# The first blocks of an encoder layer in an order held on every engine: pieces of 256 and 384 columns, three weights, zeros ahead

## The chip, the core and the metric

One core of a Trainium2 chip runs the whole kernel. The metric is the device time of one execution in microseconds (us). PE is the matrix engine (PEld its weight loads), DVE the vector engine, ACT the scalar engine, POOL the general one, and SP the engine whose queue issues the DMAs. Each engine takes its instructions in the order in which they stand in its queue.

## What is computed

One layer over 1024 prompt rows and 128 sample rows (8 streams of 16), 1152 rows of 1024 numbers in float32. The start, which the change is about, is the norm and the input projection:

```python
h = rmsnorm(x, g_pre_mix)
p = h @ w_in                       # 4352 columns
qa, ka, va, qb, kb, vb, ga, gb = jnp.split(p, cuts, axis=-1)
...
oa = prompt_band(qa, ka, va, ...)  # window attention, 8 heads on 2 KV heads
ob = prompt_band(qb, kb, vb, ...)  # chunk-band attention, 8 heads
merged = jax.nn.sigmoid(ga) * (oa @ w_oa) + jax.nn.sigmoid(gb) * (ob @ w_ob)
x = x + rmsnorm(merged @ w_out, g_post_mix)
f, conv_new = conv_ffn(rmsnorm(x, g_pre_ffn), conv_buf, w_upg, conv_w, conv_b, w_down)
return x + rmsnorm(f, g_post_ffn), ...
```

## The kernel before

Rows are taken in nine blocks of 128 (tb 0 to 8; the last holds the samples). For each block the beginning does the same seven things: a load of x (512 KB), a square with its sum on ACT (L162), the reciprocal root on POOL in two small instructions (L103, L104), the scaled block xn on DVE (L165), eight transposes on PE into two PSUM tiles `tp` (L135), and for each of these a high part of hT on ACT (L137) and a low part on DVE (L138). Operands are kept as a rounded high part and the rest, so each product is three: high by high, high by low, low by high (`mm3`, L125 to L127). A weight of 1024 x 128 is loaded raw, its high part is made on ACT (L108) and its low part on DVE (L111).

hT is held in two parts: part 0 is blocks 0 to 4 (640 columns), part 1 blocks 5 to 8 (512), each as two tiles of four k-blocks. A projection of one weight is done in three pieces of columns, `PIECES`: 320 and 320 of part 0, and 512 of part 1. A piece is 24 products into one PSUM tile, which ACT evacuates (L226; for a gate weight L302). The weights are ka and va, then q0, then for each of eight units of attention those of the next unit, with pieces of 16 gate weights (g0 to g15) dealt out over the units by `gates_per_unit`. Inside a unit the steps of attention and the dense pieces alternate. After the attention come the second merge, the output projection, and the convolutional MLP with a fast matrix scheme.

The order on each engine is made by a scheduler from the program's text and its dependences. In the kernel before it is free everywhere, and it takes ka and va alone into the beginning; the biases (`bias_tables`, one small product of PE, L533) and the constants on POOL and DVE stand where it puts them. `piece`, `weight_tile`, `split_w` and `transpose_to` are the helpers that the change touches.

```python
for g in range(NP):
    run(first[g], first[NP + g])
    if g == 0:
        bias_tables()
run(*first[2 * NP:])
```

`first` holds the pieces of ka, va and q0; `run` records all of a piece at once.

Of the kernel before, what the change touches and what calls it, by code (L numbers as in the profile page):

```python
# [11 lines left out]
F32 = mybir.dt.float32  # L12
F32R = mybir.dt.float32r
# [5 lines left out]
P = 128  # L19
D = 1024  # L20
# [24 lines left out]
def fr(ap):  # L45
    return ap.bitcast(F32)
# [3 lines left out]
def encoder_step(ctx, tc, x, w_in, w_o, w_out, w_upg, w_down, kc, vc, state_conv, conv_w, conv_b,  # L50
# [50 lines left out]
    def rstd_of(ss, out, eng=nc.vector):  # L101

        eng.tensor_scalar(out, ss, 1.0 / D, EPS, op0=ALU.mult, op1=ALU.add)  # L103
        nc.gpsimd.tensor_tensor(out, out, nhalf[:, 0:out.shape[1]], op=ALU.pow)  # L104

    def split_w(raw, sp, hi_engine="scalar", lo_engine="gpsimd"):
        if hi_engine == "scalar":
            nc.scalar.activation(sp[:, 0], raw[:], AF.Copy)  # L108
        else:
            nc.vector.tensor_copy(sp[:, 0], raw[:])  # L110
        getattr(nc, lo_engine).tensor_tensor(sp[:, 1], raw[:], fr(sp[:, 0]), op=ALU.subtract)  # L111

    def weight_tile(src, name, hi_engine="scalar"):
        raw = wr.tile([P, KD, P], F32, name=f"{name}r", tag="wr")
        nc.sync.dma_start(raw[:], src)
        sp = ws.tile([P, 2, KD, P], F32R, name=f"{name}s", tag="ws")
        split_w(raw, sp, hi_engine, "vector")
        return sp

    def mm3(ps, w, x, cols, k0, nk, start=True, stop=True):  # L120

# [7 lines left out]
    def transpose_to(pool_ps, src, dst, tb):  # L129

        s, c = part_of(tb)
        for q in range(2):
            pt = pool_ps.tile([P, 4, P], F32, name=f"tp{tb}_{q}", tag="pt")
            for k in range(4):
                nc.tensor.transpose(pt[:, k], src[:, (4 * q + k) * P:(4 * q + k + 1) * P], ident[:])  # L135
            hi = dst[s][q][:, 0, :, c:c + P]
            nc.scalar.activation(hi, pt[:], AF.Copy)  # L137
            nc.vector.tensor_tensor(dst[s][q][:, 1, :, c:c + P], pt[:], fr(hi), op=ALU.subtract)  # L138
# [6 lines left out]
    with ExitStack() as ph:  # L145
# [5 lines left out]
        early = {}  # L151
        with ExitStack() as pre:
            xp = pre.enter_context(tc.tile_pool(name="xp", bufs=3))
            xs = pre.enter_context(tc.tile_pool(name="xs", bufs=1))
            gp = xs.tile([P, D], F32, name="gp")
            nc.scalar.dma_start(gp[:], bass.AP(tensor=g_pre_mix.tensor, offset=g_pre_mix.offset, ap=[[0, P], [1, D]]))
            for tb in range(NT):
                xt = xp.tile([P, D], F32, name=f"xt{tb}", tag="xt", bufs=6)
                nc.sync.dma_start(xt[:], x[tb])
                sq = xp.tile([P, D], F32, name=f"sq{tb}", tag="sq", bufs=2)  # L160
                st = xp.tile([P, 2], F32, name=f"st{tb}", tag="st")
                nc.scalar.activation(sq[:], xt[:], AF.Square, accum_out=st[:, 0:1])  # L162
                rstd_of(st[:, 0:1], st[:, 1:2], nc.gpsimd)
                xn = xp.tile([P, D], F32, name=f"xn{tb}", tag="xn")
                nc.vector.scalar_tensor_tensor(xn[:], xt[:], st[:, 1:2], gp[:], op0=ALU.mult, op1=ALU.mult)  # L165
                transpose_to(pst, xn, hT, tb)
                if tb in (2, 5):
                    name = ("ka", "va")[tb // 3]
                    early[name] = weight_tile(w_in[4 + tb // 3], name)

        stk = ph.enter_context(tc.tile_pool(name="stk", bufs=3, reuse_waits="tile"))
# [5 lines left out]
        nsink = bcast_row(per, sink, 8, "sinkb")  # L177
        sinkb = per.tile([P, 8], F32, name="sinkp")
        nc.vector.tensor_copy(sinkb[:], nsink[:])
        nc.vector.tensor_scalar(nsink[:], nsink[:], -1.0, None, op0=ALU.mult)  # L180
        srow = per.tile([P, 2, 4], F32, name="srow")
        nc.sync.dma_start(srow[:, 0], sink_rows)
        nc.vector.tensor_scalar(srow[:, 1], srow[:, 0], -1.0, None, op0=ALU.mult)

        edge = per.tile([P, 2, 4, P], F32R, name="edge")
        nc.gpsimd.memset(fr(edge[:, :, 1:3]), 0.0)

        pnz = [per.tile([P, P], F32, name=f"pnz{i}") for i in range(2)]
        vnz = per.tile([P, 4, P], F32, name="vnz")
        for t in (*pnz, vnz):  # L190
            nc.gpsimd.memset(t[:], 0.0)
        qbds = []
        for i in range(2):
            qb = per.tile([P, NSB, 2, SS], F32, name=f"qbd{i}")
            nc.gpsimd.memset(qb[:], 0.0)
            qbds.append(qb)

        class Unit:
            pass
# [4 lines left out]
        def piece(wt, g, name, evac):  # L204

            s, c, n = PIECES[g]
            ps = psd.tile([P, 512], F32, name=name, tag="d")
            for k in range(0, KD, 2):
# [83 lines left out]
        def gate_pieces(i):  # L292
            box = {}

            def run(g):
                if g == 0:
                    box["w"] = weight_tile(w_in[18 + i], f"g{i}")
# [222 lines left out]
        def bias_tables():  # L520
            rr = pp.tile([8, 2 * CLIP + 1], F32, name="rr", tag="bt")
            nc.sync.dma_start(rr[:], relrev)
            eb = pp.tile([8, EXT_B], F32, name="eb", tag="psp", bufs=3)
            nc.vector.memset(eb[:, 0:512], 0.0)
            nc.vector.tensor_scalar(eb[:, 0:512], eb[:, 0:512], rr[:, 0:1], -1.0, op0=ALU.add, op1=ALU.mult)
            nc.vector.tensor_scalar(eb[:, 512:EXT_B], rr[:, 0:EXT_B - 512], -1.0, None, op0=ALU.mult)
# [6 lines left out]
            nc.tensor.matmul(pe[0:8, 0:EXT_A], tt[:], oh[:], start=True, stop=True)  # L533
            ea = pp.tile([8, EXT_A], F32, name="ea", tag="p", bufs=4)
            nc.scalar.activation(ea[:], pe[0:8, 0:EXT_A], AF.Copy, scale=-1.0)
            replicate(tab_a, ext_a, ea, EXT_A)


# [30 lines left out]
        def merge_weights(n, b, raw_pool, pool, tag):  # L569
            raw = raw_pool.tile([P, 4, P], F32, name=f"wo{n}_{b}r", tag="wr")  # L570
            nc.sync.dma_start(raw[:], w_o[n][:, 4 * b:4 * b + 4])
            sp = pool.tile([P, 2, 4, P], F32R, name=f"wo{n}_{b}", tag=tag)
            split_w(raw, sp, "scalar", "vector")
            return sp

        def merge_pieces(s):
# [37 lines left out]
        def spread(items, dense, n):  # L614

            done = 0
            for i, f in enumerate(items):
# [3 lines left out]
                    next(dense, None)  # L621
                done = upto

        first = unit_pieces(0)
        for g in range(NP):
            run(first[g], first[NP + g])
            if g == 0:
                bias_tables()
# [68 lines left out]
    def out_weights(k, pool):  # L697
        raw = pool.tile([P, D], F32, name=f"wt{k}r", tag="wr")
        nc.sync.dma_start(raw[:], w_out[k])
        sp = wp.tile([P, 2, D], F32R, name=f"wt{k}")  # L700
        split_w(raw, sp, "scalar", "vector")
        w_rows.append(sp)

    def split_rows(tb):
# [867 lines left out]
```

## Time and profile before

| | us |
|---|---|
| time, median of 3 runs (1675.65 to 1676.99) | 1676.21 |
| the profiled execution | 1678.73 |
| its span on the core | 1676.9 |
| PE busy in the span | 1633.9 |
| DVE, ACT, POOL busy | 1118.5, 778.5, 323.7 |
| granted PE clock, mean | 0.996 |

The span lies 1.8 us inside the profiled execution's own time, and that execution took 2.5 us more than the median. A row of a timeline gives the start, the duration, the engine, the line and the operation, the output and inputs, the count, and in brackets how long the engine had been idle before it and what ended that. A row of a group gives the count, the busy time and the mean of one in ns, then the idle time before them and its releasers. The duration of a matmul overlaps that of the next one.

### The profile page before, as it was taken

To read this page: it belongs to the slowest core of one execution; us is meant where nothing else is said; L and a number is where in the kernel's file an instruction comes from. 1 tells how busy PE (TensorE), PEld (TensorE's weight loads), DVE (VectorE), ACT (ScalarE), POOL (GpSimd) and SP (SyncE) were. 2 spreads that over 40 slices of the span, in tenths; PEclk is the share of its full clock that TensorE was granted. 3 is DMA by queue.
4 is the path that set the end of the run, shared out by engine and by line. 5 is a ranking of instruction groups with operands and counts; after the bars stand their busy time and mean duration, and the time that the engine had idled before them with its cause. 6 is when DMAs were issued, how large, how long until landed. Compare 5 with 4: busy or idle time off the path is not lost.

```text
span 1676.9 us, 28180 instructions
## 1 busy us (share of the span) xinstructions
PE 1633.9 (97%) x10559; PEld 1500.9 (90%) x10559; DVE 1118.5 (67%) x2135; ACT 778.5 (46%) x1628; POOL 323.7 (19%) x314
## 2 busy tenths in 40 slices
PE   6999999999999999999999999999999999999996
PEld 5899889999999999888899999999999997788875
DVE  6455664555556478763477766767676779888786
ACT  5344543444444455435575444445444455433332
POOL 3000000000000000000102322332223222655523
PEclk9999999999999999999999999999999999999999
DMA  5632233333323254752212222223232248443327
GB/s 192 199 100 83 77 103 97 96 95 95 88 84 101 85 157 147 227 181 100 88 59 91 86 98 92 98 97 113 92 98 97 87 158 281 145 143 127 101 74 202
DMA packets 101272, 198.57 MB, mean 118 GB/s; under 512 B 16984, under 2 KB 32904, under 8 KB 101136
## 3 DMA queue, kind: packets, MB, share of 16 engines
q1 hardware_dynamic: 99552, 191.53, 36.1%
q0 software_dynamic: 1152, 4.19, 1.4%
q8 instruction: 83, 1.36, 0.3%
q10 hardware_dynamic: 432, 1.05, 0.2%
q14 instruction: 53, 0.43, 0.1%
HBM read 139.97 MB, written 55.70 MB: 117 GB/s over the span
## 4 chain that ended last, share of the span: by engine, by line
PE 82%; DVE 8%; ACT 3%; issue 2%; DMA 2%; POOL 1%; SPq 0%; DVEq 0%; POOLq 0%; ACTq 0%
PE pa_B L978 12%; PE pc_T L978 8%; PE a L1326 5%; PE pb_B L978 4%; PE pb_T L978 4%; PE c L1326 3%; PE r L859 2%; PE r L858 2%; PE r L857 2%; PE pt L402 1%; PE o L445 1%; PE o L446 1%; PE s L377 1%; PE s L1356 1%; PE d L1326 1%
## 5 line engine op out<-in xcount | busy, mean ns | idle before, releaser
L949 ACT ACTIVATE wfb<-s 128x512 fp32r<-128x512 f32 x96 | 60.8, 633 | 134.6 <-PE pa_B L978 47.2
L950 DVE TENSOR_TENSOR wfb<-s,wfb 128x512 fp32r<-128x512 f32 x96 | 79.6, 830 | 63.0 <-ACT wfb L949 61.2
L978 PE MATMUL pa_B<-xf_T,wfb 128*128 128x256 f32 (+1 forms) x840 | 114.8, 289 | 2.7 <-DVE wide L1038 2.1
L978 PEld LDWEIGHTS pa_B<-xf_T,wfb 128*128 128x128 f32 x840 | 110.7, 188 | 3.1 <-DVE wide L1038 2.3
L383 ACT ACTIVATE p<-p,m 128x256 f32<-128x256 f32 (+4 forms) x128 | 76.3, 596 | 76.7 <-DVE m L379 75.7
L1071 POOL TENSOR_TENSOR wide<-wide 128x512 f32<-128x512 f32 (+1 forms) x46 | 78.8, 1735 | 118.4 <-DVE wide L1043 106.5
L978 PE MATMUL pc_T<-xf_T,wfb 128*128 128x256 f32 (+1 forms) x552 | 77.4, 294 | 1.7 <-DVE wfb L950 1.0
L1065 DVE SCALAR_TENSOR_TENSOR wide<-wide,cw 128x640 f32<-128x640 f32 (+2 forms) x140 | 78.8, 606 | 0.4
L978 PEld LDWEIGHTS pc_T<-xf_T,wfb 128*128 128x128 f32 x552 | 74.5, 188 | 2.5 <-DVE wfb L950 1.6
L978 PE MATMUL pc_T<-xf_B,wfb 128*128 128x256 f32 (+1 forms) x552 | 76.7, 294 | 0.0
L978 PE MATMUL pb_T<-xf_T,wfb 128*128 128x256 f32 (+1 forms) x552 | 76.6, 294 | 0.0
L978 PEld LDWEIGHTS pc_T<-xf_B,wfb 128*128 128x128 f32 x552 | 74.4, 188 | 0.0
L978 PEld LDWEIGHTS pb_T<-xf_T,wfb 128*128 128x128 f32 x552 | 74.4, 188 | 0.0
L1154 POOL TENSOR_TENSOR wf<-wdB,wf 128x1024 fp32r<-128x1024 f32 x23 | 67.2, 2943 | 29.6 <-ACT wf L1153 29.6
L336 POOL MEMSET bt<- 64x64 f32 x16 | 2.7, 168 | 325.4 <-DMA bt<-ext_b 187.6
L1063 ACT ACTIVATE wide<-wide,cb,cw 128x384 f32<-128x384 f32 (+2 forms) x70 | 46.3, 694 | 37.1 <-DVE wide L1038 37.1
L1326 PE MATMUL a<-wf,z5b 128*128 128x512 f32 x240 | 57.2, 393 | 1.3 <-POOL wf L1154 1.3
L1154 POOL TENSOR_TENSOR wf<-wdt,wf 128x1024 fp32r<-128x1024 f32 x14 | 40.4, 2893 | 88.3 <-ACT wf L1153 88.3
L104 POOL TENSOR_TENSOR str<-str,nhalf 128x1 f32<-128x1 f32 x18 | 11.1, 619 | 237.8 <-issue 155.9
L1326 PE MATMUL a<-wf,z5a 128*128 128x512 f32 x240 | 57.0, 393 | 0.0
L857 PE MATMUL r<-wt,ms 128*128 128x512 f32 x144 | 56.6, 393 | 0.0
L859 PE MATMUL r<-wt,ms 128*128 128x512 f32 x144 | 56.1, 390 | 0.0
(677 smaller groups left out, 4991.1 us busy)
## 6 DMA issues: line engine op xcount, KB each, us to landing
wqb<-in_w_upg SPq DMA_DIRECT2D x91, 256.0 KB, 2.7
zf_dr<-wide SPq DMA_DIRECT2D x84, 256.0 KB, 2.2
zr<-zf_dr SPq DMA_DIRECT2D x28, 512.0 KB, 3.8
wdB<-in_w_down SPq DMA_DIRECT2D x48, 256.0 KB, 4.0
z5a<-zf_dr SPq DMA_DIRECT2D x14, 512.0 KB, 3.6
gate_dr<-gt SPq DMA_DIRECT2D x32, 160.0 KB, 2.0
xt<-in_x SPq DMA_DIRECT2D x9, 512.0 KB, 5.4
xr<-in_x SPq DMA_DIRECT2D x9, 512.0 KB, 3.6
```

Source lines behind the costliest of these rows:

```text
L383: nc.scalar.activation(p[:, 0:n], p[:, 0:n], AF.Exp, bias=least, scale=-1.0, accum_out=st.d[:, i:i + 1])
L857: nc.tensor.matmul(ps[:, h], m[:, 0, k], w_rows[k][:, 0, hs], start=k == 0, stop=False)
L858: nc.tensor.matmul(ps[:, h], m[:, 0, k], w_rows[k][:, 1, hs], start=False, stop=False)
L859: nc.tensor.matmul(ps[:, h], m[:, 1, k], w_rows[k][:, 0, hs], start=False, stop=k == KD - 1)
L949: nc.scalar.activation(t[:, 0], src, AF.Copy)
L950: eng.tensor_tensor(t[:, 1], src, fr(t[:, 0]), op=ALU.subtract)
L978: nc.tensor.matmul(ps[:, 0:w], wf[:, h, k], xf[:, l, k], start=start and k == 0 and i == 0, stop=stop and k == 3 and i == 2, skip_group_ch ...
L1063: nc.scalar.activation(out, src(0), AF.Identity, bias=cb[:, f:f + 1], scale=cw[:, f, 0:1])
L1065: v.scalar_tensor_tensor(out, src(t), cw[:, f, t:t + 1], out, op0=ALU.mult, op1=ALU.add)
L1071: (v if pr.i < NE else p).tensor_tensor(c, c, pr.g[:, tokens(s)], op=ALU.mult)
L1154: (v if b == 0 or b == NB - 1 and i in (2, 3, 4) else p).tensor_tensor(t[:, 1], src[:], fr(t[:, 0]), op=ALU.subtract)
L1326: nc.tensor.matmul(ps[:], z[:, a, k, t * P:(t + 1) * P], w[:, b, k], start=start and k == 0 and i == 0, stop=k == 1 and i == 2, skip_group ...
```

## The change

The beginning is written out in one order by hand, and the instructions in it are recorded with `held` (the scheduler keeps recorded instructions of one engine in the order of the text). In it:

- `PIECES` becomes 256 and 384 columns of part 0; the first piece needs blocks 0 and 1 only. All later uses of the pieces follow (projections, merges).
- A third weight, g0, joins ka and va, so its three gate pieces leave the units, and units 3, 4 and 5 get 5 pieces in place of 6.
- Within a piece of the beginning the first half of k is done first for all kinds of products (high by high, then the two others, that with the operand which is made last at the end), then the second half. Between the halves a block may be turned.
- Products of zeros of 512 columns stand ahead: 14 before the first transposes, 4 and 2 further on.
- gp is loaded by SP behind the first two blocks of x, va's high part is made by POOL instead of ACT, and the constants and bias tables stand behind block 6.

```diff
-PIECES = [(0, 0, 320), (0, 320, 320), (1, 0, 512)]
+PIECES = [(0, 0, 256), (0, 256, 384), (1, 0, 512)]
...
+        if pool_high:
+            hold(nc.gpsimd.tensor_copy(sp[:, 0], raw[:]))
...
+        def sums(tb):
+            ...
+            held(nc.scalar.activation(sq[:], xts[tb][:], AF.Square, accum_out=st[:, 0:1]))
+            held(nc.gpsimd.tensor_scalar(st[:, 1:2], st[:, 0:1], 1.0 / D, EPS, op0=ALU.mult, op1=ALU.add))
+            held(nc.gpsimd.tensor_tensor(st[:, 1:2], st[:, 1:2], nhalf[:, 0:1], op=ALU.pow))
...
+        warm(14)
+        load_x(0)
+        load_x(1)
+        gp = bcast_row(xs, g_pre_mix, D, "gp")
+        wk = weight_rows(w_in[4], "ka")
...
+        turned(0)
+        scaled(1)
+        early["ka"] = weight_split(wk, "ka", hold=held)
+        wg = weight_rows(w_in[18], "g0")
+        load_x(5)
+        warm(4)
+        turned(1)
+        warm(2)
+        for q in range(2):
+            for tb in range(2):
+                high(tb, q)
+                low(tb, q)
+        sums(2)
...
+                late = ((1, 0), (0, 1)) if name[0] == "k" or g else ((0, 1), (1, 0))
+                for q in range(2):
+                    for i, (a, b) in enumerate(((0, 0), *late)):
...
+        early["va"] = weight_split(wv, "va", hold=held, pool_high=True)
+        run(first[0])
+        sums(3)
+        scaled(2)
+        sums(4)
...
+        turned(4)
+        for q in range(2):
+            high(3, q)
+            high(4, q)
+        for q in range(2):
+            for tb in (2, 3, 4):
+                low(tb, q)
...
+        now = first[NP + 1]()
+        next(now)
+        scaled(6)
+        turned(6)
+        for _ in now:
+            pass
+        normed(6)
+        sums(7)
...
+        bias_tables()
+        now = gates[1]()
+        next(now)
+        scaled(7)
+        turned(7)
+        for _ in now:
+            pass
+        normed(7)
+        sums(8)
+        scaled(8)
+        turned(8)
+        normed(8)
+        run(gates[2])
...
-        gates_per_unit = [9, 6, 6, 6, 6, 6, 7, 2]
+        gates_per_unit = [9, 6, 6, 5, 5, 5, 7, 2]
```

`normed(tb)` is the two high parts and then the two low parts of a block; `now` is a piece, of which `next(now)` records the first half and the loop the second half with its evacuation.

In the rows below, `sq` is a square, `hT_127` to `hT_130` are the four tiles of hT, `tp_0` and `tp_1` the two PSUM tiles of a turned block, `kap`, `vap`, `g0p` the PSUM tiles of pieces, and `gt` an evacuated gate piece. ACT at the end of the beginning, before:

```order
L162 ACTIVATE sq_324,st_325<-xt_322 128x1024
L137 ACTIVATE hT_129<-tp_0_280 128x4x128
L137 ACTIVATE hT_130<-tp_1_287 128x4x128
L162 ACTIVATE sq_347,st_348<-xt_345 128x1024
L137 ACTIVATE hT_129<-tp_0_308 128x4x128
L137 ACTIVATE hT_130<-tp_1_315 128x4x128
L137 ACTIVATE hT_129<-tp_0_331 128x4x128
L137 ACTIVATE hT_130<-tp_1_338 128x4x128
L226 ACTIVATE karaw<-kap_406 128x320
```

The same place now:

```order
L277 ACTIVATE varaw<-vap_460 128x384
L195 ACTIVATE hT_129<-tp_0_475 128x4x128
L195 ACTIVATE hT_130<-tp_1_480 128x4x128
L177 ACTIVATE sq_502,st_503<-xt_404 128x1024
L586 ACTIVATE ea<-pe 8x384
L353 ACTIVATE gt_1_596<-g0p_559 128x384
L195 ACTIVATE hT_129<-tp_0_574 128x4x128
L195 ACTIVATE hT_130<-tp_1_579 128x4x128
L177 ACTIVATE sq_603,st_604<-xt_406 128x1024
L195 ACTIVATE hT_129<-tp_0_610 128x4x128
```

Before, the squares of blocks 7 and 8 (the first and fourth row) stand ahead of all evacuations of pieces; now each stands behind the evacuation of a piece of 384 columns and the high parts of the block ahead of it.

PE there, before (blocks 6, 7 and 8 turned within va's first piece):

```order
L135 MATMUL tp_0_308<-ident,xn_306 128x128 x4
L135 MATMUL tp_1_315<-ident,xn_306 128x128 x4
L127 MATMUL vap_433<-hT_127,vas 128x320
L135 MATMUL tp_0_331<-ident,xn_329 128x128 x4
L135 MATMUL tp_1_338<-ident,xn_329 128x128 x4
L125 MATMUL vap_433<-hT_128,vas 128x320
```

PE now, from block 4 to half of the piece behind block 7:

```order
L191 MATMUL tp_0_384<-ident,xn_340 128x128 x4
L191 MATMUL tp_1_389<-ident,xn_340 128x128 x4
L253 MATMUL kap_418<-hT_127,kas 128x384 x12
L191 MATMUL tp_0_433<-ident,xn_431 128x128 x4
L191 MATMUL tp_1_438<-ident,xn_431 128x128 x4
L253 MATMUL kap_418<-hT_128,kas 128x384 x12
L253 MATMUL vap_460<-hT_127,vas 128x384 x12
L191 MATMUL tp_0_475<-ident,xn_473 128x128 x4
L191 MATMUL tp_1_480<-ident,xn_473 128x128 x4
L253 MATMUL vap_460<-hT_128,vas 128x384 x12
L584 MATMUL pe<-oh,tt 8x384
L253 MATMUL g0p_559<-hT_127,g0s 128x384 x12
```

A late block is now turned behind half a piece or more, and dense products of the same queue stand behind it.

DVE at blocks 2 to 5, before, where the low parts of a block stand together:

```order
L165 SCALAR_TENSOR_TENSOR xn_278<-xt_271,st_274,gp 128x1024
L138 TENSOR_TENSOR hT_127<-tp_0_234,hT_127 128x4x128
L138 TENSOR_TENSOR hT_128<-tp_1_241,hT_128 128x4x128
L138 TENSOR_TENSOR hT_127<-tp_0_257,hT_127 128x4x128
L138 TENSOR_TENSOR hT_128<-tp_1_264,hT_128 128x4x128
```

And now:

```order
L116 TENSOR_TENSOR g0s<-g0r,g0s 128x1024
L183 SCALAR_TENSOR_TENSOR xn_340<-xt_192,st_294,gp 128x1024
L199 TENSOR_TENSOR hT_127<-tp_0_312,hT_127 128x4x128
L199 TENSOR_TENSOR hT_127<-tp_0_357,hT_127 128x4x128
L199 TENSOR_TENSOR hT_127<-tp_0_384,hT_127 128x4x128
L199 TENSOR_TENSOR hT_128<-tp_1_317,hT_128 128x4x128
L199 TENSOR_TENSOR hT_128<-tp_1_362,hT_128 128x4x128
L183 SCALAR_TENSOR_TENSOR xn_431<-xt_223,st_409,gp 128x1024
```

The low parts of blocks 2, 3 and 4 (tiles 312, 357, 384) are now taken by halves of k, so that of block 2's second half (`tp_1_317`) stands behind that of block 4's first (`tp_0_384`). There are four PSUM tiles for turned blocks, so `tp_1_389` takes the place of `tp_1_317`.

More of the change, by code (lines that the diff above doesn't have):

```diff
@@ L185, in encoder_step @@
[L185 to L196, printed above, removed]
+        pre = ExitStack()
@@ new lines, in high, with low, warm @@
+        def high(tb, q):
+            s, c = part_of(tb)
+            held(nc.scalar.activation(hT[s][q][:, 0, :, c:c + P], pts[tb, q][:], AF.Copy))
+        def low(tb, q):
+            s, c = part_of(tb)
+            held(nc.vector.tensor_tensor(hT[s][q][:, 1, :, c:c + P], pts.pop((tb, q))[:], fr(hT[s][q][:, 0, :, c:c + P]),
+                                         op=ALU.subtract))
+        def warm(n):
+            ps = pss.tile([P, 512], F32, name="zero", tag="s")
+            for _ in range(n):
+                held(nc.tensor.matmul(ps[:], zeros[:, 0:P], zeros[:], start=True, stop=True))
@@ L622, in spread, with normed @@
                 done = upto
-        first = unit_pieces(0)
[L625 to L628, printed above, removed]
+        def normed(tb):
+            for q in range(2):
+                high(tb, q)
+            for q in range(2):
+                low(tb, q)
+        first = unit_pieces(0)
+        early["va"] = weight_split(wv, "va", hold=held, pool_high=True)
[3 more added lines that the diff above has]
+        sums(4)
@@ new lines, in encoder_step @@
+        now = first[NP]()
+        next(now)
+        turned(2)
+        scaled(3)
+        early["g0"] = weight_split(wg, "g0", xs, hold=held)
+        for _ in now:
+            pass
+        scaled(4)
+        for q in range(2):
+            high(2, q)
+        now = gates[0]()
+        next(now)
+        turned(3)
+        for _ in now:
+            pass
+        load_x(6)
+        turned(4)
+        for q in range(2):
+            high(3, q)
+            high(4, q)
+        for q in range(2):
+            for tb in (2, 3, 4):
+                low(tb, q)
@@ new lines, in encoder_step @@
+        load_x(7)
+        load_x(8)
+        sums(5)
+        sums(6)
+        now = first[1]()
+        next(now)
+        scaled(5)
+        turned(5)
+        for _ in now:
+            pass
+        normed(5)
+        now = first[NP + 1]()
+        next(now)
+        scaled(6)
+        turned(6)
+        for _ in now:
+            pass
+        normed(6)
+        sums(7)
+        nsink = bcast_row(per, sink, 8, "sinkb")
+        sinkb = per.tile([P, 8], F32, name="sinkp")
+        held(nc.vector.tensor_copy(sinkb[:], nsink[:]))
@@ new lines, in encoder_step @@
+        held(nc.vector.tensor_scalar(nsink[:], nsink[:], -1.0, None, op0=ALU.mult))
+        srow = per.tile([P, 2, 4], F32, name="srow")
+        nc.sync.dma_start(srow[:, 0], sink_rows)
+        held(nc.vector.tensor_scalar(srow[:, 1], srow[:, 0], -1.0, None, op0=ALU.mult))
+        edge = per.tile([P, 2, 4, P], F32R, name="edge")
+        held(nc.gpsimd.memset(fr(edge[:, :, 1:3]), 0.0))
+        pnz = [per.tile([P, P], F32, name=f"pnz{i}") for i in range(2)]
+        vnz = per.tile([P, 4, P], F32, name="vnz")
@@ new lines, in encoder_step @@
+        for t in (*pnz, vnz):
+            held(nc.gpsimd.memset(t[:], 0.0))
+        qbds = []
+        for i in range(2):
+            qb = per.tile([P, NSB, 2, SS], F32, name=f"qbd{i}")
+            held(nc.gpsimd.memset(qb[:], 0.0))
+            qbds.append(qb)
+        bias_tables()
+        now = gates[1]()
+        next(now)
+        scaled(7)
+        turned(7)
+        for _ in now:
+            pass
+        normed(7)
[3 more added lines that the diff above has]
+        normed(8)
@@ L629, in encoder_step @@
+        run(gates[2])
+        pre.close()
+        stk = ph.enter_context(tc.tile_pool(name="stk", bufs=3, reuse_waits="tile"))
+        gates = gates[3:]
+        run(first[NP + 2])
+        pts = None
+        run(first[2])
         run(*first[2 * NP:])
```

100 lines of the change are left out of this document (56 added, 44 removed).

## The prediction

> **What bounds the kernel now.** I read the stretches first, then the start in order of time, then the durations of its groups. The columns of a stretch are its bounds, its length, the busy time (count) of PE, PEld, DVE, ACT and POOL, the clock that PE was granted, the DMA share and GB/s.
>
> ```profile
> 0.00:10.00 10.00, 0.00 (x0) 0.00 (x0) 0.68 (x3) 4.61 (x7) 2.43 (x12) 1.00 0.78 295
> 10.00:20.00 10.00, 7.76 (x31) 6.76 (x32) 9.51 (x11) 8.49 (x16) 6.76 (x13) 1.00 1.04 393
> 20.00:30.00 10.00, 7.62 (x47) 7.31 (x47) 8.15 (x11) 6.48 (x12) 3.71 (x6) 1.00 0.15 53
> 30.00:40.00 10.00, 10.00 (x61) 9.09 (x60) 7.90 (x14) 4.71 (x9) 1.07 (x1) 0.83 0.20 57
> 40.00:50.00 10.00, 10.00 (x58) 9.12 (x57) 0.00 (x0) 0.88 (x2) 0.00 (x0) 1.00 0.76 209
> ...
> 300.00:350.00 50.00, 50.00 (x327) 46.40 (x326) 26.29 (x82) 22.15 (x59) 1.04 (x3) 1.00 0.35 103
> ```
>
> From 30 us on PE has no gap worth naming, so the kernel lasts as long as PE's work and the time PE loses at the start. A microsecond lost there is a microsecond at the end. The whole forecast is therefore one difference: the time PE loses before it runs dense, before and after.
>
> ```profile
> 5.94 1.06 ACT L162 ACTIVATE sq<-xt 128x1024 f32<-128x1024 f32 x1 [3.50 <-DMA xt<-in_x]
> 7.62 1.06 ACT L162 ACTIVATE sq<-xt 128x1024 f32<-128x1024 f32 x1 [0.52 <-DMA xt<-in_x]
> 8.97 1.06 ACT L162 ACTIVATE sq<-xt 128x1024 f32<-128x1024 f32 x1 [0.21 <-DMA xt<-in_x]
> 9.87 2.48 DVE L165 SCALAR_TENSOR_TENSOR xn<-xt,st,gp 128x1024 f32<-128x1024 f32 x2 [8.46 <-POOL st L104]
> 10.19 1.06 ACT L108 ACTIVATE kas<-kar 128x1024 fp32r<-128x1024 f32 x1
> 11.21 4.64 PE L135 MATMUL tp<-ident,xn 128*128 128x128 f32 x20 [11.21 <-DVE xn L165]
> 17.24 0.61 PE L125 MATMUL kap<-hT,kas 128*128 128x320 f32 x1
> 29.52 0.42 PE L127 MATMUL vap<-hT,vas 128*128 128x320 f32 x1 [2.38 <-DVE vas L111]
> ```
>
> PE first works at 11.2 us, does its first product at 17.2 and waits 2.4 us for a weight at 29.5. It also runs at two paces, which these rows show (a start to the next start is what one costs):
>
> ```profile
> 21.64 1.75 PEld L135 LDWEIGHTS tp<-ident,xn 128*128 128x128 f32 x8
> 23.63 0.94 PEld L135 LDWEIGHTS tp<-ident,xn 128*128 128x128 f32 x8
> 20.57 0.47 PE L125 MATMUL kap<-hT,kas 128*128 128x320 f32 x1
> 20.83 0.47 PE L126 MATMUL kap<-hT,kas 128*128 128x320 f32 x1
> 37.18 0.81 PE L533 MATMUL pe<-oh,tt 32*8 32x384 f32 x2
> 37.91 0.41 PE L125 MATMUL kap<-hT,kas 128*128 128x320 f32 x1
> 40.80 0.31 PE L126 MATMUL kap<-hT,kas 128*128 128x320 f32 x1
> 41.53 0.31 PE L125 MATMUL vap<-hT,vas 128*128 128x320 f32 x1
> 41.73 0.44 ACT L226 ACTIVATE karaw<-kap 128x320 f32<-128x320 f32 x1 [3.23 <-PE kap L127]
> 80.61 0.28 PE L445 MATMUL o<-ps,vsa 128*128 128x256 f32 x1
> 80.73 0.28 PE L446 MATMUL o<-ps,vsa 128*128 128x256 f32 x1
> ```
>
> A product of 320 columns costs 0.26 us slow and 0.146 fast (five of them from 40.80 to 41.53); eight transposes, one block of x by half, cost 1.75 or 0.94 for the block. At 41.53 PE has done 72 products of 320 (10.5), the transposes of 9 blocks (8.5) and the bias product (0.73): 19.7 us of full-pace work. **Lost before: 41.5 - 19.7 = 21.8 us.**
>
> **The change part by part.** *Pieces of 256 and 384.* A product of 256 costs 0.12 us (80.61 to 80.73), the same per column as one of 320, so 256 + 384 costs what 320 + 320 does, everywhere. Nothing gained or lost. *Three gate pieces* leave units 3 to 5 for the start: PE's sum is the same, and PE has no wait there that a piece less could lay bare (50.00 of 50 in 300:350). Nothing. *Late operands last* moves products inside a piece; its worth is in the chain below. *Zeros*: the 20 products do no work; 14 lie where PE was idle, six in the chain. The rest is the order, so I follow it with these durations:
>
> ```profile
> L138 DVE TENSOR_TENSOR hT<-tp,hT 128x512 fp32r<-128x512 f32 x18 | 11.9, 688 | 2.8 <-ACT hT L137 2.7
> L165 DVE SCALAR_TENSOR_TENSOR xn<-xt,st,gp 128x1024 f32<-128x1024 f32 x9 | 11.1, 1280 | 8.9 <-POOL st L104 8.9
> L111 DVE TENSOR_TENSOR kas<-kar,kas 128x1024 fp32r<-128x1024 f32 x1 | 1.2, 1218 | 0.0
> L525 DVE TENSOR_SCALAR eb<-eb,rr 8x512 f32<-8x512 f32 x1 | 0.5, 469 | 0.0
> ...
> L137 ACT ACTIVATE hT<-tp 128x512 fp32r<-128x512 f32 x18 | 10.2, 597 | 7.1 <-PE tp L135 6.6
> L162 ACT ACTIVATE sq<-xt 128x1024 f32<-128x1024 f32 x9 | 9.5, 1057 | 5.6 <-DMA xt<-in_x 4.5 <-issue 1.1
> L162 ACT ACTIVATION_READ_ACCUMULATOR sq<-xt 128x1 f32 x9 | 1.7, 193 | 0.0
> ```
>
> ```profile
> 26.61 0.19 POOL L103 TENSOR_SCALAR st<-st 128x1 f32<-128x1 f32 x1 [3.40 <-ACT sq L162]
> 26.89 0.55 POOL L104 TENSOR_TENSOR st<-st,nhalf 128x1 f32<-128x1 f32 x1
> ...
> L1154 POOL TENSOR_TENSOR wf<-wdB,wf 128x1024 fp32r<-128x1024 f32 x23 | 67.2, 2943 | 29.6 <-ACT wf L1153 29.6
> L191 POOL MEMSET vnz<- 128x512 f32 x1 | 0.5, 516 | 0.0
> ```
>
> *Up to the fifth block.* gp now shares SP's queue as the third load of 512 KB; the third lands at 7.6 (the second square above: gp and two blocks), the fourth, now ka's weight, at 9.0. So xn0 runs 7.7 to 9.0, xn1 to 10.3. If PE is at full pace, block 0 is turned from 9.1 to 10.0, four zeros to 10.9, block 1 to 11.9, two zeros to 12.4. There the first product starts, 4.8 us earlier than before, and ka's 24 products of 256 last to 15.2, held back a little by the four DVE low parts (0.69 each). va's high part is now a POOL copy of 128x1024, behind the sums of block 2 at 15.5. No row shows it: the fill above, doubled to 1024, gives 1.0, the two-input operation of that size 2.9. One input lies between, so I take 2.0. In the Trainium skill, the GPSIMD Engine Reference (4.1 Engine selection) calls one-input operations there roughly line-rate; at the 1.22 of DVE's row the sum below would be 0.8 less, and no run so far shows which. After the copy DVE goes on without a gap: va's low part to 18.8, xn2 20.1, xn3 21.4, g0's low part 22.6, xn4 23.9. PE follows: va's last four of the first half to 19.4, block 2 turned 20.2 to 21.1, va's second half to 22.5, g0's first half to 23.9, block 3 to 24.9, g0's second half to **26.3**, where block 4 is turned. The work done by then is 72 products of 256 (8.4) and four blocks (3.8), so 14.1 are lost. The floor is DVE alone: five xn, three low parts of weights and four of blocks are 12.8 from 7.8 on, 20.6, or 5.7 less.
>
> *From there to the last block, counted from t = 0 at 26.3.* ACT is one queue, and its row for the finished gate piece now stands ahead of the high parts, these ahead of the next square.
> (a) Block 4's second half takes the PSUM tile of block 2's second half, which DVE's low part frees only behind the low part of block 4's first half. ACT: hand-over 0.2, evacuation 0.4, two high parts to 1.8; DVE three low parts behind them to 3.3. PE idles from 0.47 to 3.4: **2.9**.
> (b) High part to 4.7, square and its read to 5.95, POOL 0.19 + 0.55 with hand-overs to 6.8, xn5 to 8.1. PE has ka's half piece of 384 (12 x 0.175 = 2.1) until 6.0, then waits for block 5 until 8.25: **2.3**.
> (c) Block 6: ka's evacuation stands ahead of block 5's high parts, and xn6 behind its low parts: 0.2 + 0.5 + 1.2 + 0.8 + 1.4 = 4.1 against 2.1 of va: **2.0**.
> (d) Block 7: evacuation, two high parts, a low part, then on DVE the small tables (two of 0.47 and some lesser ones, 1.2 to 1.7) and xn7, together 5.6, against bias product and half a g0 piece, 2.8: **2.8**.
> (e) Block 8: 0.2 + 0.5 + 1.2 + 1.25 (square) + 0.83 (POOL) + 0.1 + 1.28 + 0.1 = 5.4, and PE has nothing else in its queue: **5.4**; then **0.4** for the first high part of block 8.
> Sum 15.8 us, beside 18.0 us of work (five blocks 4.7, six half pieces 12.6, bias product 0.73). In the order before, the last square stands ahead of six high parts, and none of these waits exists.
>
> **Lost after at full pace: 14.1 + 15.8 = 29.9, that is 8.1 more than before.**
>
> *The clock.* After the gap up to 29.5 PE was granted half its clock:
>
> ```profile
> 30.00:31.00 1.00, 1.00 (x6) 1.00 (x5) 1.00 (x2) 0.00 (x0) 1.00 (x1) 0.58 0.56 49
> 31.00:32.00 1.00, 1.00 (x5) 0.96 (x5) 1.00 (x2) 0.00 (x0) 0.07 (x1) 0.50 0.80 311
> 32.00:33.00 1.00, 1.00 (x6) 1.00 (x6) 1.00 (x1) 0.33 (x1) 0.00 (x0) 0.50 0.47 180
> 33.00:34.00 1.00, 1.00 (x8) 0.98 (x7) 0.75 (x2) 0.74 (x2) 0.00 (x0) 0.71 0.00 0
> ```
>
> 0.42 + 0.5 + 0.5 + 0.29 = 1.7 us lost for a gap of 2.4. The gap (e) is twice as long: 1.7, with the row's own price. Gaps (a) to (d), 2.0 to 2.9, are like the one seen; part of a slow piece hides in the wait behind it, so I take 1.2 for all four (0 to 5.1). The Trainium skill, TensorE: Matmul & The Clock Gate (HAM oscillation), warns of idle gaps over about 3.4 us only; by that (e) alone would pay and the sum would be 9.8. This trace shows half clock after 2.4, so the row decides. The 14 zeros at the slow pace (0.26 x 512/320 = 0.42) end near 7.4; whether the pace is full at 9.1 after a pause of 1.7 no row shows. If not, two blocks and six zeros cost 2.7 more, of which about 1.8 reach (a); I take none and keep it for the range.
>
> **Sum: +8.1 + 1.7 + 1.2 = +11.0 us.** The profiled execution took 1678.73, 2.5 over the median of the runs; on the median: 1676.2 + 11.0 = **1687.2**.
>
> **The rivals.** *No change (within 0.2%, 3.4 us, which is about what a measurement here can tell).* The start reaches DVE's floor (-5.7) and no clock price is paid (-2.9): +2.4. For it: DVE's rows of 10:20 are nearly full already. Against: the copy on POOL and the rows behind it in DVE's queue. *Faster.* If the waits (a) to (e) sum to less than 4.4 with the start at the floor (8.4 lost, 18.4 in all), the order wins 3.4 us; at 3.0 of waits it is 4.8 faster, 1671.4. That needs squares and high parts of the late blocks to run beside dense work, as before; against it stands ACT's order, where each square sits behind an evacuation of a piece that PE has just ended. *Slower by far.* PE is slow from the start (+1.8), the copy takes 2.9 (+0.9) and all gaps pay the full clock price (+3.9, and 1.7 more behind (e)): +19, 1695.5. *The change does not do what it says*: the first product not earlier than 17.2 us, which needs the slow pace at the start (12.4 + 2.7 = 15.1) and gp 2 us late besides. Then (a) starts some 4 us later, and the sum is +15, 1691.2.
>
> **How the numbers follow.** The forecast, slower by 3.4 to 14 us, 0.72; slower by far 0.10; not doing what it says 0.03; no change 0.09; faster 0.06. The first three make slower 0.85. The time is the likeliest case's sum. The range leaves out the floor and the pile of all bad bounds: 1680 to 1694.
>
> **What would show it.** First product at 12 to 15 us (right) or past 17 (wrong). PE idle ahead of the transposes, waiting for DVE's xn and hT: about 13 to 16 us past 25 us, the longest, near 5, ahead of the last block. The ninth square behind the 384-column evacuation on ACT, not ahead of it. The first 512-column product near 60 us; a forecast of "slower" fails if it starts before 52 (19.7 + 10.5 us of work and 21.8 lost). Half clock in the stretch behind it. The POOL copy between 1 and 3 us. Past that product no new wait and the same busy sums.

## The result and the profile after

The changed kernel takes 1694.31 us (median of 5 runs, 1693.14 to 1694.39) against 1676.6 (5 runs): ratio 1.0104, 95% interval 1.0089 to 1.0119. It is slower by 17.7 us; the forecast was 11.0. The profiled execution took 1693.87, its span is 1692.1. PE is busy for 1644.0 us of it, 10.1 more than before.

The stretches of the kernel after, in the columns of the prediction (bounds, length, PE, PEld, DVE, ACT, POOL, granted clock, DMA share, GB/s):

```profile
...
20.00:30.00 10.00, 7.75 (x59) 7.19 (x58) 6.50 (x9) 6.00 (x12) 2.25 (x4) 1.00 0.67 220
30.00:40.00 10.00, 7.54 (x48) 7.25 (x49) 3.29 (x4) 1.47 (x3) 1.41 (x2) 1.00 0.00 0
40.00:50.00 10.00, 7.38 (x36) 6.20 (x35) 4.36 (x9) 2.85 (x6) 2.89 (x8) 0.86 0.22 58
50.00:60.00 10.00, 5.09 (x19) 4.18 (x18) 3.96 (x5) 3.70 (x7) 0.74 (x2) 0.67 0.93 314
60.00:70.00 10.00, 10.00 (x44) 8.10 (x43) 0.00 (x0) 0.60 (x1) 0.29 (x2) 0.96 0.58 172
```

Before, PE was full from 30 us on. Now it is full only from 60 us on, and in 30:60 DVE, ACT and POOL idle for more than half of the time: no engine is saturated there, each waits for another. The timeline of PE of the same kernel shows where (start, duration, and in brackets PE's idle time ahead of the row and what ended it):

```profile
1.48 5.67 PE L206 MATMUL zero<-zeros 128*128 128x512 f32 x14 [1.48 <-DVE zeros L209]
8.74 1.09 PE L191 MATMUL tp<-ident,xn 128*128 128x128 f32 x8 [1.59 <-DVE xn L183]
11.93 3.04 PE L253 MATMUL kap<-hT,kas 128*128 128x256 f32 x24
...
24.40 0.60 PE L191 MATMUL tp<-ident,xn 128*128 128x128 f32 x4
26.25 0.66 PE L191 MATMUL tp<-ident,xn 128*128 128x128 f32 x4 [1.25 <-DVE hT L199]
...
30.95 1.06 PE L191 MATMUL tp<-ident,xn 128*128 128x128 f32 x8 [1.96 <-DVE xn L183]
...
37.69 1.09 PE L191 MATMUL tp<-ident,xn 128*128 128x128 f32 x8 [1.51 <-DVE xn L183]
...
46.54 1.34 PE L191 MATMUL tp<-ident,xn 128*128 128x128 f32 x8 [2.62 <-DVE xn L183]
47.53 3.75 PE L253 MATMUL g0p<-hT,g0s 128*128 128x384 f32 x12
56.19 1.94 PE L191 MATMUL tp<-ident,xn 128*128 128x128 f32 x8 [4.91 <-DVE xn L183]
57.96 7.16 PE L253 MATMUL g0p<-hT,g0s 128*128 128x512 f32 x24
64.96 5.66 PE L253 MATMUL vap<-hT,vas 128*128 128x512 f32 x24
```

The five bracketed waits from 26.25 to 56.19 are (a) to (e) of the prediction, in its order. The ninth square stands where it was said to stand, behind the evacuation of the 384-column gate piece, as the timeline of ACT of the kernel after shows:

```profile
51.31 0.49 ACT L353 ACTIVATE gt<-g0p 128x384 f32<-128x384 f32 x1 [7.55 <-PE g0p L253]
51.70 1.08 ACT L195 ACTIVATE hT<-tp 128x512 fp32r<-128x512 f32 x2
52.65 1.07 ACT L177 ACTIVATE sq<-xt 128x1024 f32<-128x1024 f32 x1
```

ACT had been idle for 7.55 us ahead of these rows, with the ninth block of x long loaded: only the order held its square back.

By the prediction's count the first 512-column piece starts at 57.96 behind 30.2 us of work at full pace (72 products of 256, 8.4, and of 384, 12.6; nine blocks, 8.5; the bias product, 0.73), and takes 7.0 us (57.96 to 64.96) where the next takes 5.5. Lost at the start: 27.8 + 1.5 = 29.3, against 21.8 before, so **+7.5**. This is the count of one execution: in the trace of the kernel with whole weights (below), whose held beginning is the same, the piece starts at 60.00 and takes 6.8, which gives +9.3, since there half clock follows (b) too.

That is under half of the 17.7. The rest lies where nothing was expected. The waits of PE between 100 and 760 us in the kernel after (what waited, for what: us, times, longest):

```profile
...
PE v5p L133 <- DVE v5s L116: 0.9, 1, 0.9
PE v6p L133 <- DVE v6s L116: 0.9, 1, 0.9
...
PE o L496 <- ACT edge L456: 0.4, 2, 0.2
...
```

No row for v5 or v6 stands in the same view of before. v5p and v6p are the value projections of two units, `v5s` and `v6s` their split weights. The high part of v5s on ACT, in the kernel before and then in the one after (duration min/median/max in ns, first and last start):

```profile
L108 ACT ACTIVATE v5s<-v5r x1: 1052/1052/1052, 325.5 to 325.5; 128x1024 fp32r<-128x1024 f32 x1
```

```profile
L115 ACT ACTIVATE v5s<-v5r x1: 1067/1067/1067, 357.4 to 357.4; 128x1024 fp32r<-128x1024 f32 x1
```

Before, it started 16 us ahead of its first use at 341.7. After, it starts at 357.4, 1.1 us ahead of its first use at 358.5. The timeline of PE there, after:

```profile
357.05 0.39 PE L496 MATMUL o<-edge,vs 128*128 128x256 f32 x1 [0.22 <-ACT edge L456]
...
358.48 0.39 PE L131 MATMUL v5p<-hT,v5s 128*128 128x256 f32 x1 [0.17 <-ACT v5s L115]
...
359.47 0.34 PE L132 MATMUL v5p<-hT,v5s 128*128 128x384 f32 x1
360.67 0.39 PE L133 MATMUL v5p<-hT,v5s 128*128 128x256 f32 x1 [0.86 <-DVE v5s L116]
```

A product of 384 costs 0.17, so 1.0 us is lost ahead of 360.67 alone; the splits in ACT's queue hold up the steps of attention around them as well. From the first product of k5 to that of k7, two units on, PE takes 177.1 us after (339.2 to 516.3) and 177.9 before (from 325.6). In between, after has one gate piece of 256 columns and one of 384 fewer to do, 24 x (0.117 + 0.175) = 7.0. So the units lose **+6.2**, half of it in each. (The expectations below take 6.7, from a count of PE's starts above full pace.)

The reason that the code gives: the pool of split weights has two slots, and a gate weight is needed for its three pieces. With 5 pieces to a unit, a gate weight's pieces straddle two units; its slot stays taken, the next unit's k takes the other, and v's split can only begin when k's last product is done. The split of the gate weight g9 and its use by PE, after:

```profile
L131 PEld LDWEIGHTS g9p<-hT,g9s x24: 187/188/192, 329.5 to 402.0; 128*128 128x128 f32 x24
...
L115 ACT ACTIVATE g9s<-g9r x1: 1053/1053/1053, 314.6 to 314.6; 128x1024 fp32r<-128x1024 f32 x1
```

g9s is held from 314.6 to 402, across all of k5 and v5, which take turns in the other slot; in the kernel before its products lie together, from 378.9 to 393.9. With 6 or 3 pieces to a unit both slots are free where a unit starts.

The rest of the spans' difference (15.2): two stretches of half clock late in the MLP. The stretches of the kernel after, where before shows 1.00 at the same two places:

```profile
1400.00:1410.00 10.00, 8.11 (x34) 7.00 (x35) 8.81 (x15) 6.89 (x11) 4.61 (x3) 0.83 0.84 262
1630.00:1640.00 10.00, 7.62 (x27) 5.82 (x26) 9.34 (x8) 2.42 (x3) 6.43 (x2) 0.83 0.34 105
```

0.17 of 10 us twice is 3.4. So 7.5 + 6.2 + 3.4 = 17.1, and 1.9 came back in small pieces that I did not assign. PE's lag behind the kernel before, read at the same products of both timelines (less 7.0 at k5, where after has done two gate pieces more), is 6.5 us at the first product of k5, 12.7 at that of k7, 11.5 at that of the merge (mb) and 15.2 at the end. So the losses in the units and late lie where they were put, and what came back lies ahead of k5 and between k7 and the merge. Medians differ by 17.7 since before's profiled execution lay 2.1 over its median and after's 0.4 under.

### The profile page after: what moved, and what is told of

Same layout as the page of the kernel before. It is cut to its first block, busy times and chain, and to the rows that moved or that the text cites. A ratio compares the mean times of both kernels' runs of the same rounds, so it can differ in the third digit from the quotient of the medians.

```text
span 1692.1 us, 28254 instructions
## 1 busy us (share of the span) xinstructions
PE 1644.0 (97%) x10579; PEld 1502.6 (89%) x10579; DVE 1119.2 (66%) x2136; ACT 776.0 (46%) x1627; POOL 323.7 (19%) x315
## 4 chain that ended last, share of the span: by engine, by line
PE 83%; DVE 8%; ACT 3%; issue 2%; POOL 1%; DMA 1%; DVEq 0%; POOLq 0%; ACTq 0%
PE pa_B L1117 12%; PE pc_T L1117 8%; PE a L1465 6%; PE pb_B L1117 4%; PE pb_T L1117 4%; PE c L1465 3%; PE r L996 2%; PE r L998 2%; PE r L997 2%; PE o L497 2%; PE o L496 2%; PE pt L453 2%; PE d L1465 1%; PE s L428 1%; PE s L1495 1%
## 5 line engine op out<-in xcount | busy, mean ns | idle before, releaser
L430 DVE CUSTOM_DVE_ANT_0 p<-s,bt 128x320 f32<-128x320 f32 (+2 forms) x64 | 31.1, 486 | 40.9 <-PE s L429 30.6
L996 PE MATMUL r<-wt,ms 128*128 128x512 f32 x144 | 56.8, 394 | 0.8 <-DVE gb L871 0.8
L430 DVE CUSTOM_DVE_ANT_0 p<-s,bt,sinkb 128x256 f32<-128x256 f32 (+1 forms) x64 | 29.6, 464 | 41.3 <-PE s L429 32.7
```

What stands on the lines that cost most here:

```text
L430: nc.vector.tensor_tensor_reduce(p[:, c * cw:(c + 1) * cw], ps[:, 0:cw], un.bt[:, w - n + c * cw:w - n + (c + 1) * cw], 1.0, least, ALU.ad ...
L996: nc.tensor.matmul(ps[:, h], m[:, 0, k], w_rows[k][:, 0, hs], start=k == 0, stop=False)
```

## The experiments

Each was timed beside the kernel before (its medians were 1676.8 to 1677.8). Two theories stood at first for the loss in the units. *Kept weight*: the straddling gate weight occupies a slot. *Thin cover*: a unit with 5 pieces has too little dense work to hide the splits.

**Whole weights** (the kernel after, every unit a multiple of three pieces where v5 and v6 are split):

```diff
-        gates_per_unit = [9, 6, 6, 5, 5, 5, 7, 2]
+        gates_per_unit = [9, 6, 6, 3, 6, 6, 7, 2]
```

> The changed kernel with gate pieces per unit 9, 6, 6, 3, 6, 6, 7, 2 in place of 9, 6, 6, 5, 5, 5, 7, 2, so that no gate weight is carried over the start of a unit. Theory of the kept weight: in the trace of the changed kernel v5's and v6's splits start only when k5 and k6 are done, since g9 and g11 hold one of the two slots for split weights, and units 4 and 5 lose 3.4 us each. Then this run is 6.7 us faster than the changed kernel, about 1687.6, and PE waits for no v5 or v6 weight. Rival of the thin cover: a unit with fewer dense pieces lays attention's own waits bare; then unit 3, with 3 pieces less than before, loses more than it did, and the time stays at 1694 or above.

1688.17 us (1686.66 to 1690.11), ratio 1.0065 (1.0052 to 1.0078): 6.1 less than after. The split in this kernel:

```profile
L115 ACT ACTIVATE v5s<-v5r x1: 1052/1052/1052, 334.2 to 334.2; 128x1024 fp32r<-128x1024 f32 x1
```

It is 16 us ahead of its first use (350.3) again, and PE waits for neither v5 nor v6. The fourth unit has only three pieces to hide v4's split here, and PE waits for no v4 either, which speaks against thin cover.

**The kept weight in the kernel before** (nothing of the new beginning; 5, 5 and 8 pieces):

```diff
-        gates_per_unit = [9, 6, 6, 6, 6, 6, 7, 2]
+        gates_per_unit = [9, 6, 6, 5, 5, 8, 7, 2]
```

> The kernel before with one edit: gate pieces per unit 9, 6, 6, 5, 5, 8, 7, 2 in place of 9, 6, 6, 6, 6, 6, 7, 2. Theory of the kept weight: a gate weight is carried over the starts of units 4 and 5, and each loses about 3.4 us at its v weight: 6.7 us slower than before, 1683.3. Rival of the thin cover: units 3 and 4 have one piece less and unit 5 two more, so at most units 3 and 4 lose a little, and PE's rows there had no wait at all: within 1 us of before.

1684.28 us (1682.16 to 1686.9), 1.0040 (1.0028 to 1.0053): +7.5. The waits of PE come back, in the kernel before with this one line changed:

```profile
...
PE v6p L127 <- DVE v6s L111: 1.1, 1, 1.1
...
PE v5p L127 <- DVE v5s L111: 0.8, 1, 0.8
```

The line alone makes a kernel slower by what the change lost in the units. The sixth unit has 8 pieces here, and v6 is waited for as in the kernel after, so cover is not what is missing.

**Norms ahead** (the kernel after; the squares of blocks 5 to 8 together, and each scaled block one block earlier, everything still held):

```diff
-        sums(5)
-        sums(6)
+        for tb in range(5, 9):
+            sums(tb)
...
         turned(5)
+        scaled(6)
...
-        scaled(6)
         turned(6)
+        scaled(7)
...
-        sums(7)
...
-        scaled(7)
         turned(7)
+        scaled(8)
...
-        sums(8)
-        scaled(8)
         turned(8)
```

> The changed kernel with the squares of blocks 5 to 8 together ahead of ka's second piece and each scaled block one step earlier, ahead of the evacuation of the piece before it; all else as in the changed kernel. Theory of the queue: the waits for blocks 6, 7 and 8 (1.5, 2.6 and 4.9 us in its trace) go, some 1.6 us remain ahead of the first product of 512 columns, and the two half-clock stretches between 47 and 61 us shrink or go: 8 to 11.5 us faster than the changed kernel, 1683 to 1686. Rival: ACT and DVE are simply full there, and the four squares early only push the high parts of block 5 back; then less than 3 us is won.

1683.57 us (1680.89 to 1684.73), 1.0034 (1.0022 to 1.0047): 10.7 less than after. The timeline of PE in this kernel:

```profile
43.90 1.04 PE L191 MATMUL tp<-ident,xn 128*128 128x128 f32 x8
...
46.89 1.04 PE L191 MATMUL tp<-ident,xn 128*128 128x128 f32 x8
48.85 0.44 PE L330 MATMUL vta<-ident,varaw 128*128 128x128 f32 x2 [0.92 <-DVE hT L199]
49.10 5.87 PE L253 MATMUL g0p<-hT,g0s 128*128 128x512 f32 x24
```

Blocks 7 and 8 are turned without a wait; (c), (d) and (e) are gone, with the half clock behind them. The 512-column piece starts 8.9 us earlier and runs at full pace (1.3 more). What held PE was the place of the squares in ACT's queue and of the scaled blocks in DVE's; this run moves both and does not part them.

**No zeros** (the kernel after without the 20 zero products):

```diff
-        warm(14)
...
-        warm(4)
...
-        warm(2)
```

> The changed kernel without its 20 products of zeros (left out of the work; they give nothing to the output). Theory of the clock: PE then runs at the slow pace (0.22 us for a product of 256) until some 5 us of dense work are done, about 16 to 18 us from the start, so blocks 0 and 1 and most of ka's first piece cost twice as much: some 4 us more of PE time less 1.4 us of zeros that stood in the chain; va's weight waits anyway, so 1 to 3 us slower than the changed kernel, 1695 to 1697. Rival: the zeros are all hidden or idle either way, and the time stays within 0.5 us, or falls by 1.4.

1694.95 us (1694.63 to 1695.77), 1.0104 (1.0090 to 1.0118): +0.6, less than the 1 to 3 expected, and by the ratios no difference from after. The timeline of PE without zeros:

```profile
8.88 3.67 PE L191 MATMUL tp<-ident,xn 128*128 128x128 f32 x16 [8.88 <-DVE xn L183]
12.39 3.79 PE L250 MATMUL kap<-hT,kas 128*128 128x256 f32 x24
...
24.92 0.60 PE L191 MATMUL tp<-ident,xn 128*128 128x128 f32 x4
```

PE runs slow until about 14 us: ka's first piece costs 3.8 instead of 3.0. But block 4 is turned at 24.92 against 24.40. The zeros do what they are for, and the chain of copies and scaled blocks on POOL and DVE behind them takes almost all of it back.

**Pieces alone** (the kernel before with 256 and 384 columns):

```diff
-PIECES = [(0, 0, 320), (0, 320, 320), (1, 0, 512)]
+PIECES = [(0, 0, 256), (0, 256, 384), (1, 0, 512)]
```

> The kernel before with the pieces of 256 and 384 columns alone (no other edit). Theory: a product costs the same per column in both sizes, so nothing changes: within 1.5 us of before. Rival: the unequal pieces disturb attention's steps or the merges, which would give the changed kernel a second loss in the units: 3 us slower or more.

1677.31 us (1676.66 to 1680.45), 0.9999 (0.9990 to 1.0008): nothing, as the prediction had it.

**Three mends** (after, with whole weights and norms ahead, and the low parts of blocks 2 to 4 block by block, which was to take wait (a) away):

```diff
-        for q in range(2):
-            for tb in (2, 3, 4):
+        for tb in (2, 3, 4):
+            for q in range(2):
                 low(tb, q)
```

> The changed kernel with three mends: the gate pieces of the run with whole weights (9, 6, 6, 3, 6, 6, 7, 2), squares and scaled blocks ahead as in the run with the norms ahead, and the low parts of blocks 2, 3 and 4 by block in place of by half, so that block 4's second half has its PSUM tile at once. If the losses stand apart and add: 1694.3 - 6.1 - 10.7 - 1.3 = 1676.2, the time of before, with PE losing some 18 us at the start in place of before's 21.8, and only the chance of half-clock stretches late in the kernel on top. Rival: one of the mends takes up what another gave (DVE or ACT full at the start), and it stays above 1680.

1676.21 us (1673.52 to 1679.07), 0.9989 (0.9980 to 0.9999). The mends add up: 18.1 less than after, 6.1 and 10.7 of it from the two above. Wait (a) is gone; PE waits for 0.58 us for a high part behind block 4 instead.

**Block 5 ahead too** (the same, with its square and its scaled block ahead of block 4's turn):

```diff
+        sums(5)
...
+        scaled(5)
         turned(4)
...
-        scaled(5)
         turned(5)
```

> The run with three mends, and block 5's square and scaled block ahead of the low parts of blocks 2 to 4 too. The wait of 2.0 us for block 5 goes: about 1674, which is 0.1 to 0.2% faster than before. Rival: the low parts of blocks 2 to 4 come 1.3 us later instead, and ka's second piece waits for them: no gain over the run with three mends.

1674.51 us (1671.89 to 1675.55), 0.9975 (0.9966 to 0.9985): (b) goes as well, for a wait of 0.97 us ahead of block 4. The 512-column piece starts at 45.96, against 46.66 with three mends.

**Free order** (the text of the kernel after, but the scheduler orders what `held` had fixed):

```diff
-        held = tc.keep_in_program_order
+        held = lambda ins: ins
```

> The changed kernel with the same text, but no order held: the scheduler orders the beginning. It then puts the squares of blocks 5 to 8 ahead of the evacuations, all 20 zeros ahead, and keeps gate pieces 5, 5, 5. Theory of the queue: the waits for blocks 7 and 8 go as in the run with the norms ahead, 1683 to 1686. Rival: pieces and third weight cost the time whoever orders them, and it stays above 1690.

1675.74 us (1674.47 to 1676.31), 0.9983 (0.9975 to 0.9992): 18.6 less than after, and 7 to 10 better than I expected. I had taken the scheduler to do about as well as the two norms ahead; at the start it does better than all my edits by hand (45.96), though it still carries the kept weight. The timeline of ACT in this kernel:

```profile
18.70 1.06 ACT L177 ACTIVATE sq<-xt 128x1024 f32<-128x1024 f32 x1
...
22.00 1.08 ACT L177 ACTIVATE sq<-xt 128x1024 f32<-128x1024 f32 x1
...
23.30 1.09 ACT L177 ACTIVATE sq<-xt 128x1024 f32<-128x1024 f32 x1
```

The last squares are done by 24.5, where the held order did the ninth at 52.65. The timeline of PE, the same kernel:

```profile
37.88 1.03 PE L191 MATMUL tp<-ident,xn 128*128 128x128 f32 x8
...
40.87 1.03 PE L191 MATMUL tp<-ident,xn 128*128 128x128 f32 x8
41.74 0.38 PE L330 MATMUL vta<-ident,varaw 128*128 128x128 f32 x2
42.16 5.87 PE L253 MATMUL g0p<-hT,g0s 128*128 128x512 f32 x24
```

Lost at the start: 42.2 - 30.2 = 12.0, which is 9.8 less than before and 17.3 less than in the held order.

**Free order and whole weights** (both one-line edits):

> The run with the free order and, in addition, gate pieces 9, 6, 6, 3, 6, 6, 7, 2. Theory: the two losses of the changed kernel are apart; the kept weight's 6.1 to 6.7 us go here too, and it comes to 1669 to 1670, 0.4 to 0.5% faster than before. Rival: the free order in the units had already hidden part of it; then it stays above 1673.

1670.89 us (1670.04 to 1672.18), 0.9963 (0.9950 to 0.9977): 4.9 less than free order alone, the third measurement of the kept weight. Each taken against the kernel before that it was timed beside (6.1 and 2.1 less), it is 4.0; in the two traces the stretch from k4's first product to k7's takes 244.4 and 251.1 us, 6.7 less.

**The same without zeros**:

> The run with free order and whole weights without the 20 products of zeros (left out of the work). With the norms ahead nothing later hides a slow start: PE reaches the full pace at 5.4 us with zeros, and without them only after about 5 us of dense work, near 15 to 18 us. Blocks 0 and 1 and ka's first piece then cost double, some 3 to 4 us, of which DVE's own chain hides a part: 1 to 3 us slower than the run with zeros. Rival: DVE's chain hides all of it, and the zeros are worth nothing (within 0.7 us), as they were in the held order.

1670.60 us (1669.93 to 1670.78), 0.9959 (0.9947 to 0.9972). I expected a loss of 1 to 3 us; there is none. PE is slow until 15 us, yet the 512-column piece starts at 42.87 against 42.54. With or without zeros this version is 6 us faster than the kernel before and 23 to 24 faster than the kernel after; between the two there is no difference that these runs can tell.

## Why the prediction was wrong

The direction, the place and the mechanism at the start were right. The time missed the range by 0.3 us and the forecast by 7.1 (the difference, 17.7, by 6.7), because one step failed, and one that was too large hid part of it.

- **"Three gate pieces leave units 3 to 5 ... Nothing": failed.** It cost 6.1 (taken out of after), 7.5 (put into before) and 4.0 to 4.9 (taken out of free order). I checked that PE had no wait in 300:350 that a piece less could lay bare, and so looked for lost cover alone. What changed was not the amount of work but the phase: 5 is no multiple of three, and a weight held across the start of a unit keeps one of two slots. The row to look at was the lead of a split over its first use (325.5 against 341.7), and the question to ask of it what frees the slot.
- **The start, +11.0: right in kind, 3.5 too large.** Block 4 was turned at 24.40, not 26.3, so 1.9 less was lost there; waits (a) to (e) came to 1.25, 1.96, 1.51, 2.62 and 4.91, together 12.25 against 15.4. In (a) I had named the wrong tile: PE went on at 26.25, when the first of DVE's five low parts from 25.51 on had ended, and that is the one of block 3's first half, two ahead of the part that I took to free PE's tile. So by the time of its release `tp_1_389` waited for `tp_0_357`, and not for `tp_1_317` as the section on the change has it. In the other direction the clock took 4.0 (1.7 behind (d), 2.3 behind (e)) where I had 2.9.
- **The POOL copy, 2.0 taken: too long.** The timeline of POOL, after:

```profile
14.20 0.55 POOL L179 TENSOR_TENSOR st<-st,nhalf 128x1 f32<-128x1 f32 x1
14.70 1.04 POOL L113 CAST vas<-var 128x1024 fp32r<-128x1024 f32 x1
```

  The end of my bounds by the doubled fill, 1.0, was the right one. By the rule of the Trainium skill that I weighed (GPSIMD Engine Reference, 4.1 Engine selection) the copy ran at roughly line rate; the measured 1.04 agrees with it, and is under DVE's 1.22.
- **The clock: right that short gaps are paid.** Half clock began at 47.19 behind the gap of 2.62 us at (d), not only behind the 4.91 of (e). The rule of the Trainium skill that only gaps over about 3.4 us count (TensorE: Matmul & The Clock Gate, HAM oscillation) does not hold in this trace. But (a), (b) and (c), 1.25 to 1.96, were free in this execution.
- **"Past that product no new wait and the same busy sums": wrong**, by the waits for v5 and v6, and by the 3.4 us of late half clock, which the kernel has in some executions and to which I gave no term.
- **Pieces of 256 and 384, nothing: right** (0.9999). **The zeros: that they cost nothing was right**, and PE was at full pace behind them (block 0 turned in 1.09). But my price of a slow start without that pace, 1.8 by (a), was too high: without zeros block 4 is turned 0.5 later, since the chain behind them waits for DVE and POOL anyway.
- **The rival "faster" named its own condition rightly**: the squares and high parts of the late blocks running beside dense work. The change as it stands does not meet it; the same text with a free order does. Its limit of 4.4 us for the waits was summed wrongly: 18.4 in all less 8.4 at the floor leaves 10.0.
- **The rival "slower by far", +19, came nearest to 17.7, by luck**: of its three conditions none was met (PE was not slow from the start, the copy took 1.04, and of the first four gaps only (d) was paid). Luck as well is that the kernel with whole weights, which lacks the step that failed, lies 11.4 over before, close to the 11.0: its start and its clock differ from the sum in both directions.

Shown by experiment: the kept weight (three ways), the place of the squares and the scaled blocks (together, by norms ahead), zeros and pieces. The free order agrees, but it moves more than these. Argued only: that a taken slot is what holds back v's split (by the code and g9s's rows), which of the executions meet the late half clock, and the 1.9 us that came back.

## What to carry to other kernels

An order fixed by hand needs the off-path steps (here squares and scaled blocks) as early as their data allows, since any of them that stands behind an evacuation of the bounding engine's result can make that engine wait for itself; try the scheduler's own order of the same text before fixing it. When work is moved out of a loop, check what holds a buffer over each boundary, not only how much work is left: count the pieces that share a loaded operand against the pieces of a stage. Products that only raise the clock were worth nothing here, where another engine's chain sets the pace behind them.

## What the runs showed of the hardware

The granted clock switches on a grid. In the clock records of the kernel after, the switches lie at 47.19, 50.60, 54.02, 60.84, 1402.28, 1405.69, 1634.39 and 1637.80 us, each 3.41 us or a whole multiple of it from the next; the other traces have the same step, and the phase of the grid differs from run to run. Whether a gap is paid with a stretch of half clock (3.41 us, 1.7 lost) then varies. In the MLP, PE has the same gap of 2.4 us in every kernel, for the same input, ending between 1612 and 1635. The stretch that holds it in the kernel with norms ahead:

```profile
1620.00:1630.00 10.00, 7.61 (x34) 5.83 (x33) 9.98 (x9) 2.53 (x3) 6.57 (x2) 1.00 0.35 105
```

And in the kernel with three mends:

```profile
1610.00:1620.00 10.00, 7.60 (x26) 5.78 (x25) 9.13 (x8) 2.19 (x3) 6.22 (x2) 0.83 0.33 105
```

The same idle time, 1.00 in one and 0.83 in the other. The same holds at the start: (b) was free in the profiled execution of the kernel after, where the eight transposes behind it take 1.06, and paid in that of the kernel with whole weights, whose timeline of PE has

```profile
31.38 1.58 PE L191 MATMUL tp<-ident,xn 128*128 128x128 f32 x8 [1.96 <-DVE xn L183]
```

Ahead of block 0, a gap of 2.30 us was paid in the kernel with norms ahead (its eight transposes took 1.97), and one of 2.84 was free in the one with whole weights (1.09). So a gap of 2 to 3 us has no fixed price here; it was 0 in one execution and 1.7 us in another.

What fits all twelve traces is PE's busy time within a stretch of the grid, counted from the records behind each trace's first clock record. Each stretch in which PE was busy for 0.43 of it or less was followed by half clock: 0.23 ahead of 47.19, 0.43 ahead of the paid (b), 0.30 at the MLP's gap with three mends. Each with more than half was followed by the full clock: 0.67 and 0.76 around the free (b), 0.53 at the MLP's gap with norms ahead. Between 0.43 and 0.5 both occurred. So the phase would decide by how it parts a gap over two stretches; that is argued from these counts, since no run set the phase.
